# Stage 1 of a two-branch attention block: half a gate unit moved behind the scores, a z unit in the values' bank, the fourth query tile read and normalised last

## The chip, the cores and the metric

The kernel runs on one core of one Trainium2 chip. The metric is the time of one execution on the device in microseconds (us). The core has five engines, each with an instruction queue of its own: PE (TensorE, matmuls), DVE (VectorE), ACT (ScalarE), POOL (GpSimd) and SP (SyncE, which here issues DMAs). An engine takes its instructions in order; an instruction that waits for another engine holds all that stand behind it. Matmuls write to PSUM, which here has eight banks of 128 x 512 fp32.

## The reference

One decoder block: u is the normalised input; one projection of it gives the inputs of an MLA and a FoX attention (16 heads each), two z gates and two merge gates. 16 meta tokens stand ahead of 512 tokens. Cut to what matters:

```python
h = jnp.concatenate([meta_tokens, x], axis=1)                 # 528 positions, d_model 1024
u = rmsnorm(h, pre_norm_g[l])
proj = u @ w_in[l]
(cq, ckv, k_pe_raw, z_mla, fq, fk, fv, f_logit, z_fox, gate_a, gate_b) = jnp.split(proj, split_idx, axis=-1)
...
o_mla = causal_block_attention(q_m, k_m, v_mla, MLA_SCALE)
y_mla = (o_mla * jax.nn.silu(z_mla)) @ w_br_mla[l]
cum = jnp.cumsum(log_sigmoid(f_logit + fox_forget_b[l]), axis=-1)
o_fox = causal_block_attention(fox_heads(fq), fox_heads(fk), fox_heads(fv), FOX_SCALE, cum)   # + cum[t] - cum[s]
y_fox = (o_fox * jax.nn.silu(z_fox)) @ w_br_fox[l]
mixed = (jax.nn.sigmoid(gate_a) * y_mla + jax.nn.sigmoid(gate_b) * y_fox) @ w_out[l]
h = h + rmsnorm(mixed, post_norm_g[l])
return h[:, N_META:]
```

## The kernel before

Every fp32 product is made of three matmuls on split operands: an operand is written as a high part and a low part, and wh x uTh, wh x uTl and wl x uTh are summed in PSUM. A weight of a unit comes by DMA (`wraw`, 128 x 1024), ACT casts it to the high part (`wh`, L131), and a subtraction gives the low part (`wl`, L104), on POOL as a rule; in stage 1 alone two units have it on DVE (`low[0]=nc.vector` in the code). `wraw`, `wh` and `wl` have three buffers each.

After a start-up (norm, small projections, the values of the first pair) come 16 stages: for each of eight pairs of heads first FoX, then MLA. A stage computes the attention of its two heads; its free TensorE time is filled with units that later stages need. Units are named by their tile: `pg` is a merge gate (24 matmuls: eight steps of three), `z` a z gate (24), `mq` and `mk` MLA's queries and keys, `fq` and `fk` FoX's, `v` values. A `z` unit ends with ACT's tanh and a DVE product into `sil`, a `v` unit with two reductions on DVE (L698), a scale, and copies to `vh`.

Within a stage the work goes like this. PE makes the scores `st` of four query tiles of 128 (tile b has 144 + 128 b keys, so tile 3 is the largest): tile 1 and the first 240 keys of tile 3 share one pair of banks (one for each head), tile 0 and the rest of tile 3 the next, tile 2 has a pair alone. DVE evicts the scores to SBUF (`sf`), adding the bias or mask, and keeps a running minimum `nb` (L792; each eviction is followed by a read of its accumulator, shown as a second row with `nb` alone). ACT takes the exponentials and their sums `su` (L800). DVE scales and inverts the sums (L807, L808, into `ri`): a group of tiles 0 to 2 (six columns) and one of tile 3 (two). ACT writes the normalised high parts in f16 to `pn` (L826), DVE the low parts (L827), POOL the 16 meta columns (L813 to L818, by way of `mt`). SP issues four DMA transposes `pt<-pn`, one for a tile. When all four have landed, PE runs the 26 values matmuls `ov`, after the scores of the next stage.

PSUM's eight banks: three for `acc` (units, and tiles 1 and 3 of the scores), four by name (`b0`, `b1`, `c0`, `c1`: the rest of the scores, keys, values), one for `ov`.

PE's order is the order in which the code is written. That of the other engines is set by a scheduler when the kernel is built, from dependencies and priorities; `tc.high_priority` raises an instruction, and `tc.issue_after(x)` places what follows behind x. `weights(...)` splits each unit into a load, a preparation (`prep`: cast and subtraction) and the matmul steps, which `run(...)` writes out. Stage 1 (si == 0 in the code) is written by hand: gate unit, scores, z, then the rest.

Of the kernel before, what the change touches and what calls it, by code (L numbers as in the profile page):

```python
# [55 lines left out]
def block_kernel(ctx: ExitStack, tc: tile.TileContext, x, meta_tokens, pre_norm_g, w_in, fox_forget_b,  # L56
# [485 lines left out]
    with ExitStack() as att:  # L542
# [7 lines left out]
        def bank(tag):  # L550
            return lambda name: stp.tile([128, 512], F32, tag=tag, name=name)

        def two(tag):
            return lambda name: bank(tag + name[-1])(name)

# [18 lines left out]
        for b in range(4):  # L574
            nc.gpsimd.memset(pn[b // 3][:, PN_STEP * b % 15], 0.0)
        gT = []
        masks, normed = [], []

        wuqh = wuq.rearrange("p k (h e) -> p k h e", e=NOPE + ROPE)

# [148 lines left out]
        def z_unit(br, pr):  # L729
            def done(i, pz):  # L730
                sil = aw.tile([128, S], F32, tag="sil", name=f"sil{br}{pr}")
                with tc.high_priority(offset=60), nullcontext() if pr or not br else tc.issue_after(normed[0]):
                    ins = nc.scalar.activation(sil, pz, AF.Tanh, scale=0.5)
                    nc.vector.scalar_tensor_tensor(out=sil, in0=sil, scalar=1.0, in1=pz, op0=ALU.add, op1=ALU.mult)
                if written[0] and not br:

                    behind.append(ins.ins)
                sils[br, pr] = sil
            return unit(f"z{br}{pr}", win_w((O_ZM, O_ZF)[br], pr), u_act, KD, REAL, done)

        def attention(br, pr):


            scale = (SC_MLA, SC_FOX)[br]
            nm_ = f"{br}{pr}"
            q, k = hls["q", br, pr], hls["k", br, pr]

# [17 lines left out]
            def added(h, b, c0, c1):  # L765
# [3 lines left out]
                d = META + 128 * b if b else 0  # L769
                return [(a, e, cb[n][h][:, a:e]) for n, a, e in ((0, c0, min(c1, d)), (1, max(c0, d), c1)) if a < e]  # L770

            def scores():

                for t in ("nb", "su", "ri"):
                    sums[t] = aw.tile([128, 2, 4], F32, tag=t, name=f"{t}{nm_}")
                for g in range(2):
                    sfs[g] = aw.tile([128, 2, (2 * SF_STEP + 400, L)[g]], F32, tag=f"sf{g}", name=f"sf{nm_}{g}", bufs=1)
                for rooms, parts in (([acc, acc], ((1, 0, 272, 0), (3, 0, CUT, 272))),
                                     ([bank("b0"), bank("b1")], ((0, 0, 144, 0), (3, CUT, L - CUT, 144))),
                                     ([bank("c0"), bank("c1")], ((2, 0, 400, 0),))):  # L780
                    ps = [room(f"st{nm_}{parts[0][0]}{h}") for h, room in enumerate(rooms)]
                    for b, c0, w, o in parts:
                        for i, ops in enumerate(zip(*(sets(h, b, c0, w) for h in range(2)))):
                            for h, (Q, K) in enumerate(ops):
                                mm(ps[h][:, o : o + w], Q, K, start=(i == 0), stop=(i == last_set))
                    for b, c0, w, o in parts:
                        for h in range(2):
                            nb = sums["nb"][:, h, b : b + 1]
                            for a, e, in1 in added(h, b, c0, c0 + w):

                                with tc.high_priority(offset=100):
                                    nc.vector.tensor_tensor_reduce(  # L792
                                        out=sf_of(h, b)[:, a:e], in0=ps[h][:, o + a - c0 : o + e - c0],
                                        in1=in1, scale=-scale, scalar=3.0e38 if a == 0 else nb,
                                        op0=ALU.add, op1=ALU.min, accum_out=nb)
                with tc.high_priority(offset=60):
                    for b in (1, 0, 2, 3):
                        for h in range(2):
                            sf = sf_of(h, b)
                            exps[b // 3] = nc.scalar.activation(sf, sf, AF.Exp, bias=sums["nb"][:, h, b : b + 1],  # L800
                                                                scale=-1.0, accum_out=sums["su"][:, h, b : b + 1]).ins

            def norm(g):
                def fn():
                    b0, nb_ = GRP[g][0], len(GRP[g])
                    su, ri = (sums[t][:, :, b0 : b0 + nb_] for t in ("su", "ri"))
                    nc.vector.tensor_scalar(out=su, in0=su, scalar1=1.0 / PSCALE, scalar2=None, op0=ALU.mult)  # L807
                    nc.vector.reciprocal(ri, su)  # L808
# [4 lines left out]
                    nc.gpsimd.tensor_tensor(out=mt, in0=src, in1=ri.unsqueeze(3).broadcast_to([128, 2, nb_, META]),  # L813
                                            op=ALU.mult)
                    hi, lo, hi2 = (dst[:, :, :, 32 * i : 32 * i + META] for i in range(3))
                    nc.gpsimd.tensor_copy(hi, mt)
                    lead[:] = [nc.gpsimd.tensor_tensor(out=lo, in0=mt, in1=hi, op=ALU.subtract).ins]
                    nc.gpsimd.tensor_copy(hi2, mt)  # L818
                    for b in GRP[g]:
                        for h in range(2):  # L820
                            sf = sf_of(h, b)[:, META:].rearrange("p (j c) -> p j c", c=128)
                            t0 = PN_STEP * (b % 3) + 1
                            hi, lo = (pn[g][:, t0 : t0 + 2 * b + 2, h].rearrange("p (j l) c -> p j l c", l=2)[:, :, i]
                                      for i in range(2))
                            rib = sums["ri"][:, h, b : b + 1]
                            normed[:] = [nc.scalar.activation(hi, sf, AF.Copy, scale=rib).ins]  # L826
                            nc.vector.scalar_tensor_tensor(out=lo, in0=sf, scalar=rib, in1=hi, op0=ALU.mult,  # L827
                                                           op1=ALU.subtract)
                    for b in GRP[g]:
                        t0, n = PN_STEP * (b % 3), 2 * b + 3  # L830
                        dma(ptt[:, 0 : 2 * n, 128 * b : 128 * b + 128], pn[g][:, t0 : t0 + n].rearrange("p t h c -> p (t h c)"),
                            nc.sync.dma_start_transpose)
                return fn

            def values():
                po = ovp.tile([128, 512], F32, tag="ov", name=f"ov{nm_}")
# [93 lines left out]
        run(first[len(pe0) : -KD])  # L930
        behind[:] = [halved[("k", 1, 0), 1]]
        run(first[-KD:])
        behind.clear()
        late = []
        for si, (br, pr) in enumerate(stages):
# [6 lines left out]
                fn()  # L942
            if si == 0:

                run(fill[:1])
                run(vts[1, 0] + pe_rest)
                n0()
                bias(1)
                low[0] = nc.vector
                for ahead_ in [fn.prep for _, fn in fill[1:] if hasattr(fn, "prep")][:2]:  # L950
                    ahead_()
                low[0] = nc.gpsimd
                n1()
                run(fill[1:])
            else:
                if si == 1:
                    stores(2, 4)
# [361 lines left out]
```

## Time and profile before

| what | before |
|---|---|
| median of 3 runs | 590.39 us (590.29 to 591.79) |
| profiled execution | 589.93 us |
| its span, first to last instruction | 587.9 us |
| granted TensorE clock | 0.998 |
| PE busy | 577.0 us, 98% |
| DVE, ACT, POOL busy | 416.7, 357.2, 200.4 us |
| time of the chain that ended last on PE | 90% |

All times of single rows are microseconds from the start of the span of the profiled execution. A row of the timeline gives start, length, engine, line, operation, output <- inputs, shapes and how many instructions it stands for; brackets give the engine's idle time ahead of it and what ended it. A row with a count over 1 stands for neighbours, and its length is that from the first start to the last end. The two numbers after a tile name in the order listings are numbers of buffers and mean nothing else. Stage 1's scores start at 61.69 us and stage 2's at 77.93 us.

### The profile page before, as it was taken

How to read it: one execution, taken by the hardware profiler on the slowest of the kernel's cores; microseconds unless marked ns; L12 is line 12 of the kernel's file. 1: busy time of each engine (PE TensorE's matmuls, PEld its weight loads, DVE VectorE, ACT ScalarE, POOL GpSimd, SP SyncE). 2: the span in 40 equal slices, each digit the busy share in tenths (PEclk: the TensorE clock that was granted, in tenths of full speed). 3: DMA queues.
4: the chain of work that ended last, by engine and by line, in shares of the span. 5: the costliest groups of instructions: out<-in, count | busy, mean ns of one | idle time of the engine just before them, and what ended most of it. 6: DMA issues, size and time to landing. Idle time of an engine off the chain costs nothing.

```text
span 587.9 us, 11120 instructions
## 1 busy us (share of the span) xinstructions
PE 577.0 (98%) x3841; PEld 497.4 (85%) x3841; DVE 416.7 (71%) x1155; ACT 357.2 (61%) x816; POOL 200.4 (34%) x271
## 2 busy tenths in 40 slices
PE   8999989999999999999999999999999999999996
PEld 6889879889889889888898898878998998888884
DVE  5844687784885775766758758896747876468957
ACT  7846674783783784766748748844343462443663
POOL 4317736373467472554544644510000000000000
PEclk9999999999999999999999999999999999999999
DMA  8535399999978988988977977877622534333603
GB/s 291 127 81 168 88 194 195 234 189 277 171 169 161 223 189 204 218 190 203 178 175 178 226 149 146 183 174 259 207 73 71 144 108 130 86 109 107 216 0 143
DMA packets 219999, 97.46 MB, mean 166 GB/s; under 512 B 131456, under 2 KB 209672, under 8 KB 219944
## 3 DMA queue, kind: packets, MB, share of 16 engines
q1 hardware_dynamic: 219944, 96.77, 70.3%
q8 instruction: 30, 0.49, 0.3%
q14 instruction: 25, 0.20, 0.1%
HBM read 62.36 MB, written 3.97 MB: 113 GB/s over the span
## 4 chain that ended last, share of the span: by engine, by line
PE 90%; POOL 3%; DMA 2%; DVE 2%; ACT 1%; issue 1%; SPq 0%; DVEq 0%; POOLq 0%
PE z L98 17%; PE pg L98 14%; PE v L98 8%; PE x L98 8%; PE fq L98 8%; PE fk L98 8%; PE py L98 7%; PE st L98 7%; PE ov L98 5%; PE psm L98 3%; PE y L98 2%; PE mq L98 2%; POOL wl L104 1%; DMA pt<-pn 1%; PE mk L98 1%
## 5 line engine op out<-in xcount | busy, mean ns | idle before, releaser
L104 POOL TENSOR_TENSOR wl<-wraw,wh 128x1024 fp32r<-128x1024 f32 (+2 forms) x62 | 120.2, 1946 | 112.6 <-ACT wh L131 78.6
L131 ACT CAST wh<-wraw 128x1024 fp32r<-128x1024 f32 (+1 forms) x72 | 74.7, 1041 | 61.0 <-PE py L98 16.8
L800 ACT ACTIVATE sf<-sf,nb 128x272 f32<-128x272 f32 (+3 forms) x128 | 72.7, 569 | 10.9 <-DVE nb L792 10.1
L104 DVE TENSOR_TENSOR wl<-wraw,wh 128x512 fp32r<-128x512 f32 (+1 forms) x54 | 51.2, 950 | 31.9 <-ACT wh L1056 20.0
L827 DVE SCALAR_TENSOR_TENSOR pn<-sf,ri,pn 128x512 f16<-128x512 f32 (+3 forms) x128 | 71.5, 625 | 2.4 <-ACT pn L826 2.4
L826 ACT ACTIVATE pn<-sf,ri 128x512 f16<-128x512 f32 (+3 forms) x128 | 59.6, 548 | 0.0
L98 PE MATMUL z<-uTh,wh 128*128 128x512 f32 x128 | 51.1, 399 | 0.0
L98 PE MATMUL pg<-uTh,wh 128*128 128x512 f32 x128 | 50.1, 391 | 0.0
L98 PE MATMUL z<-uTl,wh 128*128 128x512 f32 x128 | 50.1, 391 | 0.0
L98 PE MATMUL z<-uTh,wl 128*128 128x512 f32 x128 | 50.0, 391 | 0.0
L98 PE MATMUL pg<-uTl,wh 128*128 128x512 f32 x128 | 49.9, 390 | 0.0
L98 PE MATMUL pg<-uTh,wl 128*128 128x512 f32 x128 | 49.8, 389 | 0.0
L98 PE MATMUL st<-hlk,hlq 64*128 64x272 f32 (+4 forms) x480 | 41.3, 299 | 0.0
L1056 ACT CAST wh<-wraw 128x512 fp32r<-128x512 f32 x28 | 17.3, 619 | 38.6 <-DVE wraw L1065 14.3
L698 DVE TENSOR_REDUCE vsc<-v 128x1 f32<-128x272 f32 (+1 forms) x32 | 13.1, 431 | 38.1 <-PE v L98 38.1
L98 PE MATMUL v<-uTh,wl 128*128 128x256 f32 (+1 forms) x128 | 36.5, 286 | 0.0
L98 PE MATMUL fk<-uTl,wh 128*128 128x256 f32 (+1 forms) x128 | 36.5, 285 | 0.0
L98 PE MATMUL v<-uTl,wh 128*128 128x256 f32 (+1 forms) x128 | 36.5, 285 | 0.0
L98 PE MATMUL fk<-uTh,wh 128*128 128x256 f32 (+1 forms) x128 | 36.4, 285 | 0.0
L98 PE MATMUL fk<-uTh,wl 128*128 128x256 f32 (+1 forms) x128 | 36.4, 285 | 0.0
L98 PEld LDWEIGHTS st<-hlk,hlq 64*128 64x128 f32 x480 | 33.0, 186 | 4.1 <-ACT vh L717 2.1
L98 PE MATMUL v<-uTh,wh 128*128 128x256 f32 (+1 forms) x128 | 36.4, 285 | 0.0
(285 smaller groups left out, 1611.6 us busy)
## 6 DMA issues: line engine op xcount, KB each, us to landing
wraw<-in_w_in_dram SPq DMA_DIRECT2D x56, 512.0 KB, 4.4
cbp<-c_dram SPq DMA_DIRECT2D x16, 264.0 KB, 3.7
wraw<-in_w_br_fox_dram SPq DMA_DIRECT2D x8, 512.0 KB, 4.3
tb<-in_w_out_dram SPq DMA_DIRECT2D x8, 512.0 KB, 5.2
wraw<-in_w_br_mla_dram SPq DMA_DIRECT2D x8, 512.0 KB, 4.2
wraw<-in_w_out_dram SPq DMA_DIRECT2D x6, 512.0 KB, 3.6
xr<-in_x_dram SPq DMA_DIRECT2D x4, 512.0 KB
out_dram<-yo SPq DMA_DIRECT2D x8, 256.0 KB, 2.0
```

The lines of the kernel that those rows point to most:

```text
L98: nc.tensor.matmul(*a, **k)
L104: return eng.tensor_tensor(out=lo, in0=src, in1=f32(hi), op=ALU.subtract)
L131: nc.scalar.copy(wh[:, :n], raw[:, :n])
L698: nc.vector.tensor_reduce(out=sc[:, i : i + 1], in_=ps, op=ALU.max, axis=AX.X, apply_absolute_value=True)
L800: exps[b // 3] = nc.scalar.activation(sf, sf, AF.Exp, bias=sums["nb"][:, h, b : b + 1], scale=-1.0, accum_out=sums["su"][:, h, b : b + 1]).ins
L826: normed[:] = [nc.scalar.activation(hi, sf, AF.Copy, scale=rib).ins]
L827: nc.vector.scalar_tensor_tensor(out=lo, in0=sf, scalar=rib, in1=hi, op0=ALU.mult, op1=ALU.subtract)
L1056: nc.scalar.copy(to[0], src)
```

## The change

Everything is in stage 1, and the computation is the same.

- Of the gate unit ahead of the scores only four of eight steps stay there; the other four (12 matmuls) run behind the scores, ahead of the unit z10.
- The unit z10 (FoX's z, first pair) takes the bank of `ov` instead of one of `acc`.
- DVE evicts tiles 1, 0 and 2 first (10 evictions). Tile 3's six evictions are placed behind the reciprocal of the first group, and its exponentials on ACT behind the last high copy of the first group.
- The weight subtraction of z00 (`wl`, on DVE) is placed behind the evictions of tiles 1, 0 and 2.

The core of the diff:

```diff
-            return unit(f"z{br}{pr}", win_w((O_ZM, O_ZF)[br], pr), u_act, KD, REAL, done)
+            room = ov_bank if br and not pr else None
+            return unit(f"z{br}{pr}", win_w((O_ZM, O_ZF)[br], pr), u_act, KD, REAL, done, room)
...
+            three_first = (br, pr) == stages[0]
...
+            def evict(places):
+                for b, c0, w, o, ps in places:
+                    for h in range(2):
+                        nb = sums["nb"][:, h, b : b + 1]
+                        for a, e, in1 in added(h, b, c0, c0 + w):
+
+                            with tc.high_priority(offset=100):
+                                ins = nc.vector.tensor_tensor_reduce(
+                                    out=sf_of(h, b)[:, a:e], in0=ps[h][:, o + a - c0 : o + e - c0],
+                                    in1=in1, scale=-scale, scalar=3.0e38 if a == 0 else nb,
+                                    op0=ALU.add, op1=ALU.min, accum_out=nb)
+                return ins.ins
...
+                    if three_first:
+                        places.extend(own)
+                    else:
+                        evict(own)
+                if three_first:
+                    whole[:] = [evict([p_ for p_ in places if p_[0] < 3])]
+                exponentials((1, 0, 2) if three_first else (1, 0, 2, 3))
...
-                    nc.vector.reciprocal(ri, su)
+                    inv = nc.vector.reciprocal(ri, su)
+                    if three_first and g == 0:
+                        with tc.issue_after(inv.ins):
+                            evict([p_ for p_ in places if p_[0] == 3])
...
+                    if three_first and g == 0:
+                        with tc.issue_after(normed[0]):
+                            exponentials((3,))
...
-        first = pe0 + v + [(0, in_order)] + g
+        first = pe0 + v + [(0, in_order)] + g[:4]
+        begun = g[4:]
...
-                fill = (vts[br, pr] if pr else []) + za + q + zb[:3] + k + zb[3:5] + v + zb[5:]
+                fill = (vts[br, pr] if pr else begun) + za + q + zb[:3] + k + zb[3:5] + v + zb[5:]
...
-                run(fill[:1])
+                run(fill[:5])
                 run(vts[1, 0] + pe_rest)
                 n0()
                 bias(1)
                 low[0] = nc.vector
-                for ahead_ in [fn.prep for _, fn in fill[1:] if hasattr(fn, "prep")][:2]:
-                    ahead_()
+                for ahead_ in [fn.prep for _, fn in fill[5:] if hasattr(fn, "prep")][:2]:
+                    with tc.issue_after(whole[0]):
+                        ahead_()
                 low[0] = nc.gpsimd
                 n1()
-                run(fill[1:])
+                run(fill[5:])
```

PE, around stage 1's scores (`pg` is the gate unit, `st` are scores, the number tells the bank's tile). Before, the last gate step and the first scores:

```order
L98 MATMUL pg_857<-uTh,wh_851 128x512
L98 MATMUL pg_857<-uTl,wh_851 128x512
L98 MATMUL pg_857<-uTh,wl_852 128x512
L98 MATMUL st_889<-hlk_653,hlq_619 128x272
L98 MATMUL st_890<-hlk_653,hlq_619 128x272
```

After, the last scores, the gate unit's fifth step behind them:

```order
L98 MATMUL st_903<-hlk_653,hlq_619 128x400
L98 MATMUL st_904<-hlk_653,hlq_619 128x400
L98 MATMUL pg_857<-uTh,wh_851 128x512
L98 MATMUL pg_857<-uTl,wh_851 128x512
L98 MATMUL pg_857<-uTh,wl_852 128x512
```

The four last steps of the gate unit have moved from ahead of the 30 score matmuls to behind them; z10 follows.

DVE in stage 1, from the last evictions on (L792 is L786 after, L807/L808 are L828/L829, L827 is L851, L734 is L737). Before, where `wl_1005` of z00 stands ahead of all evictions and so is not among these rows:

```order
L792 ISA sf_887,nb_884<-st_929,cbm_707,nb_884 128x128
L792 ISA nb_884 128x1
L807 TENSOR_SCALAR su_885<-su_885 128x2
L808 RECIPROCAL ri_886<-su_885 128x2
L807 TENSOR_SCALAR su_885<-su_885 128x2x3
L808 RECIPROCAL ri_886<-su_885 128x2x3
L827 SCALAR_TENSOR_TENSOR pn_716<-sf_888,ri_886,pn_716 128x4x128
L827 SCALAR_TENSOR_TENSOR pn_715<-sf_887,ri_886,pn_715 128x128 x2
L827 SCALAR_TENSOR_TENSOR pn_715<-sf_887,ri_886,pn_715 128x2x128 x2
L827 SCALAR_TENSOR_TENSOR pn_715<-sf_887,ri_886,pn_715 128x3x128 x2
L827 SCALAR_TENSOR_TENSOR pn_716<-sf_888,ri_886,pn_716 128x4x128
L734 SCALAR_TENSOR_TENSOR sil_1041<-sil_1041,z_955 128x512
```

After, from the last eviction of tile 3 on; the reciprocal of the first group (128x2x3) stands ahead of tile 3's six evictions:

```order
L786 ISA sf_874,nb_870<-st_890,cbm_708,nb_870 128x128
L786 ISA nb_870 128x1
L104 TENSOR_TENSOR wl_1005<-wraw_855,wh_1004 128x1024
L851 SCALAR_TENSOR_TENSOR pn_715<-sf_873,ri_872,pn_715 128x128 x2
L851 SCALAR_TENSOR_TENSOR pn_715<-sf_873,ri_872,pn_715 128x2x128 x2
L851 SCALAR_TENSOR_TENSOR pn_715<-sf_873,ri_872,pn_715 128x3x128 x2
L828 TENSOR_SCALAR su_871<-su_871 128x2
L829 RECIPROCAL ri_872<-su_871 128x2
L104 TENSOR_TENSOR hlq_1053<-mq_1046,hlq_1053 128x512
L851 SCALAR_TENSOR_TENSOR pn_716<-sf_874,ri_872,pn_716 128x4x128 x2
L737 SCALAR_TENSOR_TENSOR sil_1041<-sil_1041,z_947 128x512
L104 TENSOR_TENSOR hlk_1072<-mk_1068,hlk_1072 128x272
```

The subtraction for z00 has gone from ahead of the evictions to behind them, and tile 3 (sf_874, pn_716 after) is normalised last, behind the low part of hlq.

More of the change, by code (lines that the diff above doesn't have):

```diff
@@ L551, in bank, with ov_bank @@
             return lambda name: stp.tile([128, 512], F32, tag=tag, name=name)
+        def ov_bank(name):
+            return ovp.tile([128, 512], F32, tag="ov", name=name)
         def two(tag):
@@ L576, in block_kernel @@
         gT = []
-        masks, normed = [], []
+        masks, normed, whole = [], [], []
         wuqh = wuq.rearrange("p k (h e) -> p k h e", e=NOPE + ROPE)
@@ L770, in added @@
                 return [(a, e, cb[n][h][:, a:e]) for n, a, e in ((0, c0, min(c1, d)), (1, max(c0, d), c1)) if a < e]
+            places = []
+            def evict(places):
[9 more added lines that the diff above has]
+                return ins.ins
             def scores():
@@ L781, in scores @@
                     ps = [room(f"st{nm_}{parts[0][0]}{h}") for h, room in enumerate(rooms)]
+                    own = []
                     for b, c0, w, o in parts:
+                        own.append((b, c0, w, o, ps))
                         for i, ops in enumerate(zip(*(sets(h, b, c0, w) for h in range(2)))):
@@ L785, in scores, with exponentials @@
                                 mm(ps[h][:, o : o + w], Q, K, start=(i == 0), stop=(i == last_set))
[L786 to L795, printed above, removed]
+                    if three_first:
[5 more added lines that the diff above has]
+                exponentials((1, 0, 2) if three_first else (1, 0, 2, 3))
+            def exponentials(bs):
                 with tc.high_priority(offset=60):
-                    for b in (1, 0, 2, 3):
+                    for b in bs:
                         for h in range(2):
@@ L835, in values @@
             def values():
-                po = ovp.tile([128, 512], F32, tag="ov", name=f"ov{nm_}")
+                po = ov_bank(f"ov{nm_}")
                 ph = [po[64 * h : 64 * h + 64] for h in range(2)]
@@ L929, in block_kernel @@
         gT += [gpool.tile([128, KD, S], F32, tag=n, name=n) for n in ("gT0", "gT1")]
-        run(first[len(pe0) : -KD])
+        run(first[len(pe0) : -4])
         behind[:] = [halved[("k", 1, 0), 1]]
-        run(first[-KD:])
+        run(first[-4:])
         behind.clear()
```

## The prediction

> **What bounds the kernel now.** I read the busy totals first, then the chain that ended last, then TensorE's waits in the stretch that the change touches (60 to 140 us from the span's start), and last the rows around those waits. The first line gives each engine's busy time, the second the shares of the chain, the third TensorE's waits in that stretch (total us, times, longest).
>
> ```profile
> PE 577.0 (98%) x3841; PEld 497.4 (85%) x3841; DVE 416.7 (71%) x1155; ACT 357.2 (61%) x816; POOL 200.4 (34%) x271
> PE 90%; POOL 3%; DMA 2%; DVE 2%; ACT 1%; issue 1%; SPq 0%; DVEq 0%; POOLq 0%
> PE ov L98 <- DMA pt<-pn: 2.2, 1, 2.2
> 81.17 0.35 PE L98 MATMUL st<-KPL,QP 64*128 64x400 f32 x2
> 83.73 2.04 PE L98 MATMUL ov<-pt,vp 80*64 80x512 f16 x26 [2.21 <-DMA pt<-pn]
> 124.57 0.35 PE L98 MATMUL st<-KPL,QP 64*128 64x400 f32 x2
> 124.84 2.04 PE L98 MATMUL ov<-pt,vp 80*64 80x512 f16 x26
> ```
>
> TensorE is the bound: it is busy 98% of the span, so a faster side engine is worth only the TensorE idle time that it ends. In 80 us that is a single wait: stage 1's values matmuls (ov) start at 83.73 because a transpose pt<-pn lands late. What it costs is read against the same join two stages later, which waits for nothing: there ov starts 0.27 us after the last score row (124.84 - 124.57), here 2.56 us after it (83.73 - 81.17). The excess, **2.29 us**, is all that this change can win by ending that wait.
>
> Now why the transpose is late. TensorE runs the gate unit, then the scores, then z. The last row, of the chain, is the flight of the last transpose (issue, us to landing).
>
> ```profile
> 56.13 0.40 PE L98 MATMUL pg<-uTh,wh 128*128 128x512 f32 x1
> 58.87 0.39 PE L98 MATMUL pg<-uTh,wh 128*128 128x512 f32 x1
> 61.69 2.26 PE L98 MATMUL st<-hlk,hlq 64*128 64x272 f32 x30
> 63.88 0.50 PE L98 MATMUL z<-uTh,wh 128*128 128x512 f32 x1
> 61.61 1.05 ACT L131 CAST wh<-wraw 128x1024 fp32r<-128x1024 f32 x1 [2.98 <-PE pg L98]
> 62.69 1.36 DVE L104 TENSOR_TENSOR wl<-wraw,wh 128x1024 fp32r<-128x1024 f32 x1 [3.32 <-ACT wh L131]
> 63.98 0.29 DVE L792 CUSTOM_DVE_ANT_0 sf<-st,cbp 128x144 f32<-128x144 f32 x1
> 68.97 0.08 DVE L792 DVE_READ_ACCUMULATOR2_ANT nb<- 128x1 f32 x1
> 68.28 0.72 ACT L800 ACTIVATE sf<-sf,nb 128x528 f32<-128x528 f32 x1
> 70.57 0.19 DVE L808 RECIPROCAL ri<-su 128x6 f32<-128x6 f32 x1
> 70.23 3.72 ACT L826 ACTIVATE pn<-sf,ri 128x512 f16<-128x512 f32 x8
> 70.97 3.99 DVE L827 SCALAR_TENSOR_TENSOR pn<-sf,ri,pn 128x512 f16<-128x512 f32 x8 [0.21 <-ACT pn L826]
> 74.22 0.74 DVE L827 SCALAR_TENSOR_TENSOR pn<-sf,ri,pn 128x512 f16<-128x512 f32 x1
> 77.59 6.00 DMA pt<-pn
> ```
>
> The scores end at 63.88, yet the first eviction starts only at 63.98, behind z00's weight split (wl, 62.69 to 64.05). Sixteen evictions run to 69.05, the reciprocal for tiles 0 to 2 ends at 70.76, hi and lo copies to 74.96, and the last transpose, issued at 77.59, lands 6.00 us later.
>
> **The change part by part.**
>
> *Half a gate unit behind the scores.* Twelve of 24 matmuls move: 58.87 - 56.13 = 2.74 us of TensorE work. The scores start at 61.69 - 2.74 = 58.95 and the order before and after holds the same rows, so z still starts at 63.88; on TensorE itself this costs nothing. Where scores meet waiting values the first eviction follows by 1.10 us:
>
> ```profile
> 103.11 2.26 PE L98 MATMUL st<-hlk,hlq 64*128 64x272 f32 x30
> 104.21 0.31 DVE L792 CUSTOM_DVE_ANT_0 sf<-st,cbp 128x144 f32<-128x144 f32 x1 [0.17 <-PE st L98]
> ```
>
> So the first eviction falls at 60.05, 3.93 us earlier than now. 2.74 of that is the move, the rest the weight split that stood ahead.
>
> *Tiles 1, 0 and 2 first.* Before, from first eviction to the end of that reciprocal went 70.76 - 63.98 = 6.78 us, with tile 3's two exponentials in it (0.72 each). Without them: 60.05 + 6.78 - 1.44 = 65.4; tile 3's six evictions also leave the front of DVE's queue, so this is a late bound. ScalarE then casts wh (1.05) and does the gate's tanh, 0.59 by the next row: 67.0 if none overlaps, 66.6 if the cast follows the last exponential directly. Six of the eight hi copies, about 2.5 of the 3.72 us, end at about 69.2; two exponentials with their reads take 1.5 more (70.7); hlq's cast waits for mq's last matmul at 70.99 and ends at 71.6; tile 3's two hi copies (0.6 to 0.7) end at about 72.9.
>
> ```profile
> 62.56 0.59 ACT L538 ACTIVATE th<-pg 128x512 f32<-128x512 f32 x1
> 70.60 0.39 PE L98 MATMUL mq<-cTh,wl 128*128 128x512 f32 x1
> 70.83 0.40 PE L98 MATMUL z<-uTh,wh 128*128 128x512 f32 x1
> 75.48 0.68 DVE L104 TENSOR_TENSOR hlq<-mq,hlq 128x512 fp32r<-128x512 f32 x1
> 76.76 0.76 DVE L698 TENSOR_REDUCE vsc<-v 128x1 f32<-128x272 f32 x2
> 75.65 0.28 PE L98 MATMUL v<-cTh,wl 128*128 128x256 f32 x1
> ```
>
> On DVE: six evictions from 65.4 at 5.07/16 = 0.32 each, to 67.3; the split wl 1.36, to 68.7; six lo copies at about 0.4, to 71.2; two small ones; hlq's lo (0.68) to 72.3; tile 3's two lo copies (0.74 each) to 73.8. The last transpose is issued at about 73.8 instead of 77.59 and lands at 79.8. Values are wanted at 83.73 - 2.29 = 81.44: **the 2.29 us end**, with 1.6 us to spare.
>
> *z10 in the values' bank; late frees.* Tile 3's scores hold their banks until 67.3, and the gate unit its own until its tanh. The next units that need one start at 70.83 (z00) and later, so this is hidden. The split wl, now after the evictions, is ready at 68.7 against the same 70.83: 2.1 us of cover; if that goes, TensorE waits at z00, one for one. The values at 81.44 come well behind z10's reading from that bank. SP's and POOL's rows are the same in number; POOL's four small operations on tiles 0 to 2 come ahead of tile 3's and wait for no more than they did.
>
> *What is late next.* Stage 2's values weights. DVE's backlog of stage 1 now delays v's second reduction: TensorE ends v at 75.93, the two reductions end at 77.52, and a chain of DVE and ScalarE steps leads from there to stage 2's first eviction and its reciprocals:
>
> ```profile
> 80.59 0.43 DVE L792 CUSTOM_DVE_ANT_0 sf<-st,maskt 128x272 f32<-128x272 f32 x1
> 84.99 0.17 DVE L808 RECIPROCAL ri<-su 128x2 f32<-128x2 f32 x1
> 85.30 0.24 POOL L813 TENSOR_TENSOR mt<-sf,ri 128x32 f32<-128x32 f32 x1 [2.04 <-DVE ri L808]
> 87.59 2.40 POOL L104 TENSOR_TENSOR wl<-wraw,wh 128x1024 fp32r<-128x1024 f32 x1
> 89.96 0.80 POOL L813 TENSOR_TENSOR mt<-sf,ri 128x96 f32<-128x96 f32 x1
> 91.81 2.58 POOL L104 TENSOR_TENSOR wl<-wraw,wh 128x1024 fp32r<-128x1024 f32 x1
> 94.21 0.29 PE L98 MATMUL v<-uTh,wh 128*128 128x272 f32 x1
> 94.46 0.38 PE L98 MATMUL v<-uTh,wl 128*128 128x272 f32 x1
> 87.58 2.97 DVE L827 SCALAR_TENSOR_TENSOR pn<-sf,ri,pn 128x512 f16<-128x512 f32 x1 [0.62 <-ACT pn L826]
> ```
>
> After the change DVE has caught up by then, so the second reduction (the later half of the 0.76 row) can start right behind v, about 75.97 against about 77.1: **1.11 us earlier**, and with it the eviction (79.48), the reciprocal (84.05) and POOL. From 85.30 POOL works without a gap to 94.39 and ends with the wl of stage 2's v unit. TensorE's third v matmul needs that wl: its row is 0.38 long where its neighbour takes 0.29, so it already waits 0.09. With the stall gone TensorE would be there at 94.46 - 2.29 = 92.17; POOL, 1.11 earlier, would have wl at 93.28, usable at about 93.44 (the old one ended at 94.39 and was used from 94.55, the 0.09 counted, so 0.16 later). A new wait of about 1.27 us opens at v.
>
> **Sum:** -2.29 (values' wait) + 1.27 (new wait at v) - 0.09 (the old one, in it) = -1.11 us. The profiled execution took 589.93 us, so one like it would take 588.8; the median of the runs shown is 590.39, 0.46 above, and there the forecast is 590.39 - 1.11 = **589.3 us**. The unknown in it is how far stage 2's chain moves. Below: not at all, if DVE's backlog stays, which gives no gain. Above: the eviction cannot come before the scores that it reads, which bounds the move to about 1.2 us, and POOL's rows can shorten. I take 1.11, the nearer end: between 74.96 and the second reduction at about 77.1 DVE had 2.1 us of work, of which hlq's lo (0.6 net) is done earlier after the change, so from 73.8 it is through at about 75.3, 0.6 us ahead of v's end.
>
> [...] In the last row above a lo copy of DVE took 2.97 us beside POOL's wl split (87.59, 2.40), against 0.74 for the same shape at 74.22. [...]
>
> **The rivals.**
>
> *Nearly the full gain.* If POOL's stretch shortens as well, the new wait at v shrinks. For it: in that stretch mt's 0.80 is slow beside DVE's copies; the same operation took 0.35 in stage 1:
>
> ```profile
> 70.91 0.35 POOL L813 TENSOR_TENSOR mt<-sf,ri 128x96 f32<-128x96 f32 x1 [0.39 <-DVE ri L808]
> ```
>
> That is 0.45, and 0.18 for wl at 2.40 instead of 2.58: 0.63 us, so 588.7. With no wait at v at all it would be 590.39 - 2.29 = 588.1. Against it: the same neighbours run together after the change, only shifted as a block.
>
> *No gain.* The transposes or DVE's work of stage 1 stay late by 2 us or more, or the whole of stage 2's chain hangs on something that does not move; TensorE then regains at the values what it gives back at v: 590.4. Against it: v's reductions wait for DVE alone in the rows above.
>
> *Slower: DVE and POOL lock each other in stage 1.* The split wl and eight lo copies now run from about 67 on, beside POOL's operations on tiles 0 to 2. If each of the eight lost as much as the longest of POOL's small rows there, 0.61 (pn's copy at 71.32), that is 4.9 us of DVE delay:
>
> ```profile
> 71.32 0.61 POOL L816 CAST pn<-mt 128x96 f16<-128x96 f32 x1
> ```
>
> Slack ahead of v's reduction is 0.6 us, and 1.11 of gain is to be lost first: from 1.7 us of delay on it is slower than before, from 3.5 by over 0.3%, and at 4.9 us it would be 590.39 + 3.2 = 593.6. Against it: POOL has only some 2 us of such work in all, and before the change it ran beside the same copies, which still came to 3.99 us for eight.
>
> **How the numbers follow.** Chances: forecast 0.50, nearly the full gain 0.26, no gain 0.10, slower 0.14. The likeliest's own range is 588.7 to 590.0 (a move of stage 2's chain between 0.4 and 1.2, with POOL up to 0.5 shorter). The 8-in-10 range reaches below to just under the full gain, 587.9, and above over the case without gain to 590.8; what it leaves out is most of the slower case. 0.3% of 590.4 is 1.77 us, about what a measurement of this kernel can tell from no change: the faster side is most of the second case, 0.25; the slower side most of the last one and a little for what I have not seen, 0.15; the rest, 0.60, is between.
>
> **What would show each step.** In the changed profile: scores at about 58.95 and the first eviction at about 60.05; wl of z00 on DVE behind the evictions; the last of stage 1's four transposes landing near 79.8 and no wait of ov, which starts near 81.4; stage 2's two-wide reciprocal near 84.05; TensorE's v matmul waiting about 1.2 us for POOL's wl near 92.2; stage 3's scores at about 102.0 instead of 103.11. Wrong would make it: a wait of TensorE at z00 near 70.8 for wl or a bank, lo copies in stage 1 much longer than 0.74, ov still waiting, or POOL's stretch of another length than 9.1 us.

## The result, and the profile after

The changed kernel takes 589.13 us (median of 7 runs, 588.78 to 589.51), the kernel before, run beside it, 591.15 (7 runs, 590.29 to 591.79). The ratio is 0.9974, with a 95% interval of 0.9964 to 0.9984: 1.5 us less, between 0.9 and 2.1; the two medians are 2.0 us apart. The profiled execution took 589.07 us against 589.93. Of the kernel before, one run beside the last experiments took 3271.22 us and is left out everywhere.

The page of the changed kernel, span and busy time:

```profile
span 587.1 us, 11116 instructions
PE 577.8 (98%) x3841; PEld 497.7 (85%) x3841; DVE 419.4 (71%) x1155; ACT 357.1 (61%) x816; POOL 199.0 (34%) x271
```

TensorE is still busy 98% of the span. The chain that ended last can be followed back only to 83.91 us in this profile, so its shares are not set beside those of before. TensorE's waits between 60 and 140 us, and its rows around them:

```profile
PE v L98 <- POOL wl L104: 1.1, 1, 1.1
56.31 0.40 PE L98 MATMUL pg<-uTh,wh 128*128 128x512 f32 x1
59.15 2.26 PE L98 MATMUL st<-hlk,hlq 64*128 64x272 f32 x30
61.34 0.50 PE L98 MATMUL pg<-uTh,wh 128*128 128x512 f32 x1
81.36 0.34 PE L98 MATMUL st<-KPL,QP 64*128 64x400 f32 x2
81.63 2.04 PE L98 MATMUL ov<-pt,vp 80*64 80x512 f16 x26
92.14 0.29 PE L98 MATMUL v<-uTh,wh 128*128 128x272 f32 x1
93.61 0.39 PE L98 MATMUL v<-uTh,wl 128*128 128x272 f32 x1 [1.06 <-POOL wl L104]
102.27 2.26 PE L98 MATMUL st<-hlk,hlq 64*128 64x272 f32 x30
```

The values matmuls now start 0.27 us after the last score row, and a new wait stands at stage 2's v unit, for POOL's weight split. The gate unit starts 0.18 us later than in the profile of before (56.31 against 56.13), which is start-up and not the change. Counted from that row, stage 3's scores start after 45.96 us instead of 46.98: **1.02 us** gained, and from there on both kernels run alike.

DVE, POOL and SP in stages 1 and 2 of the changed kernel:

```profile
60.17 0.31 DVE L786 CUSTOM_DVE_ANT_0 sf<-st,cbp 128x144 f32<-128x144 f32 x1 [0.60 <-PE st L98]
64.57 0.84 DVE L828 TENSOR_SCALAR su<-su 128x6 f32<-128x6 f32 x1 [1.13 <-ACT sf L821]
65.45 0.19 DVE L829 RECIPROCAL ri<-su 128x6 f32<-128x6 f32 x1
67.33 1.22 DVE L104 TENSOR_TENSOR wl<-wraw,wh 128x1024 fp32r<-128x1024 f32 x1
68.46 2.46 DVE L851 SCALAR_TENSOR_TENSOR pn<-sf,ri,pn 128x128 f16<-128x128 f32 x6
72.46 1.41 DVE L851 SCALAR_TENSOR_TENSOR pn<-sf,ri,pn 128x512 f16<-128x512 f32 x2
74.78 3.00 SPq L92 DMA_TRANSPOSE pt<-pn  x1
75.80 0.78 DVE L701 TENSOR_REDUCE vsc<-v 128x1 f32<-128x272 f32 x2 [0.65 <-PE v L98]
79.71 0.44 DVE L786 CUSTOM_DVE_ANT_0 sf<-st,maskt 128x272 f32<-128x272 f32 x1
84.14 0.17 DVE L829 RECIPROCAL ri<-su 128x2 f32<-128x2 f32 x1
84.48 0.24 POOL L837 TENSOR_TENSOR mt<-sf,ri 128x32 f32<-128x32 f32 x1 [2.13 <-DVE ri L829]
91.00 2.55 POOL L104 TENSOR_TENSOR wl<-wraw,wh 128x1024 fp32r<-128x1024 f32 x1
86.73 10.58 DVE L851 SCALAR_TENSOR_TENSOR pn<-sf,ri,pn 128x512 f16<-128x512 f32 x8 [0.60 <-ACT pn L850]
```

Stage 1's last transpose is issued at 74.78 instead of 77.59; v's reductions wait 0.65 us for TensorE, where before DVE came to them 0.83 us after v's end (76.76 against 75.93); and POOL's stretch of stage 2 runs from 84.48 to 93.55, 9.07 us without a long gap (9.09 before).

### The profile page after: what moved, and what is told of

The parts are those of the page before. It is cut to its first block, busy times and chain, and to the rows that moved or that the text cites. A ratio compares the mean times of both kernels' runs of the same rounds, so it can differ in the third digit from the quotient of the medians.

```text
span 587.1 us, 11116 instructions
## 1 busy us (share of the span) xinstructions
PE 577.8 (98%) x3841; PEld 497.7 (85%) x3841; DVE 419.4 (71%) x1155; ACT 357.1 (61%) x816; POOL 199.0 (34%) x271
## 4 chain that ended last, share of the span: by engine, by line
PE 83%; POOL 1%; issue 0%; DVE 0%; DVEq 0%; ACT 0%; POOLq 0%
PE z L98 17%; PE pg L98 14%; PE v L98 8%; PE x L98 8%; PE py L98 7%; PE st L98 7%; PE fk L98 6%; PE fq L98 6%; PE ov L98 5%; PE y L98 2%; PE mq L98 2%; PE mk L98 1%; POOL wl L104 1%; PE ppe L98 0%; POOL mt L837 0%
## 5 line engine op out<-in xcount | busy, mean ns | idle before, releaser
L851 DVE SCALAR_TENSOR_TENSOR pn<-sf,ri,pn 128x512 f16<-128x512 f32 (+3 forms) x128 | 73.6, 641 | 2.1 <-ACT pn L850 1.9
L850 ACT ACTIVATE pn<-sf,ri 128x128 f16<-128x128 f32 (+3 forms) x128 | 59.7, 548 | 0.0
```

## The experiments

My theory was the prediction's: the wait at ov is worth 2.29 us, stage 2's chain moves 1.1 us, and TensorE gives the difference back at v. The rivals were that one part alone does it, or that the two waits have nothing to do with each other. Each ratio is to runs of the kernel before on the same chip; the medians of different rows are in part of different chips. Start-up differs from one profiled execution to the next by up to 1.4 us (the gate unit started between 56.03 and 57.45), so beside the ratios this table gives, from the traces, the time from the gate unit's start to stage 3's and to stage 5's scores:

| kernel | to stage 3 | to stage 5 | median us | runs, us | ratio to before (95%) |
|---|---|---|---|---|---|
| before, profile shown above | 46.98 | 88.02 | 591.15 | 590.29 to 591.79 | 1 |
| before again | 48.53 | 89.57 | 590.66 | 589.75 to 592.78 | 1.0003 (0.9992 to 1.0014) |
| changed | 45.96 | 87.00 | 589.13 | 588.78 to 589.51 | 0.9974 (0.9964 to 0.9984) |
| changed again | 45.97 | 87.01 | 589.03 | 588.89 to 589.60 | 0.9972 (0.9961 to 0.9983) |
| half gate unit alone | 46.35 | 87.39 | 589.66 | 589.14 to 590.06 | 0.9978 (0.9969 to 0.9987) |
| tile 3 last alone | 45.96 | 87.00 | 589.09 | 588.75 to 589.88 | 0.9972 (0.9963 to 0.9982) |
| changed, fk ahead of v | 44.63 | 86.32 | 588.52 | 588.33 to 589.18 | 0.9964 (0.9951 to 0.9976) |
| changed, z10 in acc | 47.88 | 88.92 | 591.06 | 590.65 to 591.26 | 0.9994 (0.9984 to 1.0005) |
| before, later transpose | 49.21 | 90.25 | 592.92 | 591.13 to 596.76 | 1.0033 (1.0016 to 1.0051) |
| changed, later transpose | 47.64 | 89.00 | 592.48 | 591.32 to 593.61 | 1.0022 (1.0009 to 1.0035) |
| changed, v's split on DVE | 44.62 | 85.73 | 588.67 | 587.97 to 589.79 | 0.9959 (0.9944 to 0.9974) |
| tile 3 last, v's split on DVE | 45.14 | 88.66 | 589.34 | 588.21 to 591.46 | 0.9978 (0.9966 to 0.9989) |

**The kernel before again.** No edit.

> The kernel before once more, unchanged, for the spread of its runs and a second profile. The wait at stage 1's values hangs on a DMA's flight, which may differ from run to run. If that is why the runs before lie up to 1.5 us apart, the second profile shows another flight and another wait at ov (first: 6.00 us and 2.21 us) while all before ov agrees within 0.3 us. Rival: the spread is in the start-up or the tail, and the wait at ov is 2.2 us again. Ratio 1.000 either way.

The flight of the last transpose and the wait at ov were the same to 0.03 us; the idea that the DMA's flight makes the spread fell. But the second half of the rival did not hold alone either. The chain's row of that transpose, and TensorE's rows at ov:

```profile
78.93 6.01 DMA pt<-pn
85.08 3.30 PE L98 MATMUL ov<-pt,vp 80*64 80x512 f16 x26 [2.24 <-DMA pt<-pn]
```

The same 26 matmuls took 3.30 us instead of 2.04. Windows around the end of the wait, first of the profile of before, then of this one, cut where its clock changes (busy time of PE, its weight loads, DVE, ACT and POOL with counts; then the granted clock, the DMA share and GB/s):

```profile
83.00:86.00 3.00, 2.27 (x27) 1.82 (x28) 1.71 (x8) 3.00 (x11) 0.89 (x5) 1.00 1.15 342
86.00:89.00 3.00, 3.00 (x15) 2.45 (x14) 2.36 (x4) 3.00 (x7) 3.00 (x6) 1.00 1.80 105
```

```profile
82.26:85.67 3.41, 1.17 (x14) 0.69 (x12) 3.41 (x20) 3.16 (x11) 2.36 (x1) 1.00 0.84 218
85.67:89.08 3.41, 3.41 (x26) 2.61 (x21) 1.26 (x6) 3.24 (x8) 2.34 (x9) 0.50 0.75 218
89.08:92.49 3.41, 3.41 (x17) 2.82 (x16) 3.41 (x5) 3.19 (x8) 3.35 (x4) 1.00 1.38 72
```

The granted clock was 0.50 for 3.41 us where it had been 1.00, and counted from the gate unit stage 3's scores came 1.55 us later. This execution took 592.78 us, 2.85 above the other profiled one: about 1.5 from the lower clock, 1.32 in the start-up (57.45 against 56.13).

**Half the gate unit alone.** Tile 3 in the old order; z00's preparation is not tied to the evictions.

```diff
-            three_first = (br, pr) == stages[0]
+            three_first = False
...
-                    with tc.issue_after(whole[0]):
-                        ahead_()
+                    ahead_()
```

> Only the half gate unit behind the scores and z10 in the values' bank; all 16 evictions, exponentials and copies in the old order. My theory: scores near 59.1 are early enough by themselves, so ov's wait is gone; but z00's weight split now comes behind six lo copies on DVE and is ready at about 71.9 instead of 68.6, so TensorE waits about 0.5 us at z00, v's end and with it stage 2's chain are 0.5 us later, and the gain against the kernel before is about 0.5 us (ratio 0.999) instead of the full change's. Rival: tile 3 last is what ends the wait at ov; then ov waits here still for 1 us or more.

TensorE's waits in this kernel between 50 and 140 us:

```profile
PE v L98 <- POOL wl L104: 1.0, 1, 1.0
PE z L98 <- DVE wl L104: 0.2, 1, 0.2
```

ov no longer waits, z00 waits a little for its split (0.17 us in its row; stage 2's scores start 0.44 later than in the others), and stage 3 comes 0.63 us sooner than before, 0.39 later than with the whole change. The mechanism is the expected one; the rival, that tile 3's order is needed to end the wait, is out. The ratio, 0.9978, shows more gain than the 0.999 expected; the trace's 0.63 us is near the expected 0.5. What the runs have beyond the traces comes up below, with the clock.

**Tile 3 last alone.** The whole gate unit ahead of the scores.

```diff
-        first = pe0 + v + [(0, in_order)] + g[:4]
-        begun = g[4:]
+        first = pe0 + v + [(0, in_order)] + g
+        begun = []
...
-            room = ov_bank if br and not pr else None
+            room = None
```

(and the numbers that count steps, 5 back to 1 and 4 back to KD)

> Only tile 3 read and normalised last and z00's split behind the evictions; the whole gate unit ahead of the scores, z10 in a bank of acc. The scores are at 61.7 to 61.9 again. My theory: tile 3's lo copies end at about 75 and the last transpose lands at 80 to 82, so ov waits 0 to 0.6 us; DVE ends stage 1's work at about 76.2, some 0.2 to 0.5 us after v's end, so stage 2's chain gains 0.6 to 0.9 of the 1.1 us. Gain against before 0.6 to 1.0 us (ratio 0.9983 to 0.999). Rival: without the earlier scores nothing is won, ov waits as before for about 2.2 us and the ratio is 1.000.

```profile
PE v L98 <- POOL wl L104: 0.9, 1, 0.9
```

That is TensorE's only wait listed there; ov starts 0.43 us behind the last score row instead of 0.27, so that 0.16 us of its wait is left. The gain to stage 3 is the whole 1.02 us, a little over what I expected, and the ratio, 0.9972, is below the expected 0.9983 to 0.999. So each half of the change ends the wait at ov by itself, or all but 0.16 us of it, and the half gate unit adds nothing measurable to the other: what is left is set behind ov, at v. This kernel holds two edits, tile 3's order and z00's split behind the evictions; which of them it takes was not tried.

**fk's matmuls ahead of v.** In stage 2 alone, 12 matmuls of fk's second half run ahead of v.

```diff
-                fill = vts[br, pr] + q + k[:KD] + v + k[KD:]
+                n_ = KD + (4 if si == 1 else 0)
+                fill = vts[br, pr] + q + k[:n_] + v + k[n_:]
```

> The changed kernel, and in stage 2 alone half of fk's second half (12 matmuls, about 1.5 us) runs ahead of the v unit instead of behind it. My theory: what the change leaves is the 1.2 us wait of v's third matmul for POOL's weight split; with 1.5 us of other work ahead the split is in time, the wait is gone and the kernel is 1.0 to 1.2 us faster than the changed one (ratio to before 0.9955 to 0.996), unless the last transpose of stage 2, which lands about 0.2 us ahead of when values would then be wanted, becomes the next wait (then 0.3 to 0.8 us less). Rival: the wait only moves to the next unit that needs stage 2's chain, stage 3's scores or values, and the time is that of the changed kernel (ratio 0.9974).

The wait at v is gone, and stage 3's scores start 1.33 us sooner than in the changed kernel. But 0.65 of it is lost at once, and not where I looked for it (PEld are TensorE's weight loads):

```profile
101.21 2.85 PE L98 MATMUL st<-hlk,hlq 64*128 64x272 f32 x30
102.86 0.86 PEld L98 LDWEIGHTS st<-hlk,hlq 64*128 64x128 f32 x8 [0.31 <-DVE hlk L104]
102.39 0.41 DVE L104 TENSOR_TENSOR hlk<-fk,hlk 128x256 fp32r<-128x256 f32 x1
102.72 0.47 DVE L723 SCALAR_TENSOR_TENSOR vh<-v,vsc,vh 128x256 f16<-128x256 f32 x1
```

The 30 score matmuls take 2.85 us instead of 2.26. The keys' low part, done on DVE at 102.80, now comes while the scores run, and a weight load waits 0.31 us for it. The rest of the loss falls around the end of v's last copy on DVE, 103.19; that the copy is its cause is argued from this time alone. The rival was half right: half of the gain is lost at stage 3's scores, and to stage 5 0.68 us are left.

**z10 in a bank of acc.**

```diff
-            room = ov_bank if br and not pr else None
+            room = None
```

> The changed kernel with z10 back in a bank of acc. The gate unit and tile 3's scores then hold all three banks of acc when TensorE comes to z10 at about 64 us. My theory: z10 waits for the gate's tanh, which in the changed kernel ends at about 66.0, so TensorE idles some 2 us at z10; half of it comes back since the wait at v (1.1 us) shrinks, but v's end and stage 2's chain are later too, so the time is 1 to 2.5 us above the changed kernel (ratio to before 0.999 to 1.002). Rival: the bank is free in time and the values' bank was not needed; ratio 0.9974.

```profile
PE z L98 <- DVE nb L786: 1.7, 1, 1.7
PE v L98 <- POOL wl L104: 1.1, 1, 1.1
66.07 0.47 PE L98 MATMUL z<-uTh,wh 128*128 128x512 f32 x1 [1.67 <-DVE nb L786]
```

z10 waits. The profile names an eviction of tile 3, whose accumulator was read by 65.92; the gate's tanh, which I had expected, ended at 66.03, and the two are not separated. Stage 3 comes 1.92 us later than in the changed kernel: all of the wait and a little more, nothing of it comes back at v, since the delay at z10 lies ahead of v's own reductions and moves stage 2's chain with it. The values' bank is what lets the half gate unit move at no cost on TensorE.

**A later transpose, before and after.** Tile 0's transpose is issued once more (in the kernel before) or twice more (in the changed one) ahead of tile 3's, the same data to the same place.

```diff
-                    for b in GRP[g]:
+                    for b in ((0,) * 1 if br and not pr and g else ()) + GRP[g]:
```

> The kernel before, with tile 0's transpose issued a second time ahead of tile 3's in stage 1, which delays the last transpose by about 1.3 us and so lengthens TensorE's wait at ov from 2.2 to about 3.5 us. The second profile of the kernel before showed a granted clock of 0.61 for some 3 us behind the 2.2 us wait, where the first showed 1.00, and 1.54 us more to stage 3's scores. My theory: an idle stretch of 2 to 2.5 us sometimes lowers the clock, and a longer one does so more often: then nearly all runs lie 2.5 to 3.1 us above the faster half of the runs of before (about 590.1), without a second cluster 1.3 us lower. Rival: the lower clock is chance and not tied to the wait; then the runs lie 1.0 to 1.6 us above before and spread as before.

> The changed kernel with tile 0's transpose issued two more times ahead of tile 3's, so that the last transpose is issued at about 77.5 as in the kernel before, while DVE and stage 2's chain stay as early as in the changed one. My theory: ov waits again for 1.3 to 2.2 us, but then TensorE comes later to v, whose wait of 1.1 us for POOL's split shrinks to between 0 and 0.3; net 0.3 to 1.1 us above the changed kernel (ratio to before 0.998 to 1.0). Rival: the two waits add up, 1.3 to 2.2 us above the changed kernel with v's wait as long as there (ratio 1.000 or more).

TensorE's rows at ov and the windows behind, first of the kernel before with the later transpose, then of the changed kernel with it, there with ScalarE's first weight cast behind stage 2's exponentials:

```profile
84.43 3.48 PE L98 MATMUL ov<-pt,vp 80*64 80x512 f16 x26 [2.90 <-DMA pt<-pn]
84.84:88.25 3.41, 3.41 (x25) 2.58 (x22) 0.83 (x4) 2.81 (x6) 2.74 (x9) 0.50 0.94 281
```

```profile
84.26 2.04 PE L98 MATMUL ov<-pt,vp 80*64 80x512 f16 x26 [2.19 <-DMA pt<-pn]
84.00:87.00 3.00, 2.74 (x29) 2.17 (x29) 1.21 (x4) 1.50 (x6) 2.09 (x8) 1.00 0.96 257
87.14 1.05 ACT L131 CAST wh<-wraw 128x1024 fp32r<-128x1024 f32 x1 [1.65 <-DMA wraw<-in_w_in_dram]
95.65 0.39 PE L98 MATMUL v<-uTh,wl 128*128 128x272 f32 x1 [0.48 <-POOL wl L104]
```

In the first the wait grew to 2.90 us, less than I meant, and the clock was 0.50 for 3.41 us behind it; the median rose by 1.5 us (591.43 for the kernel before on that chip, 592.92 here), and only one of 12 runs lay under 592.2. That fits the expectation's size only in part: 7 of the 12 runs, not nearly all, have a mean granted clock of 0.995 or less, and the runs reach 596.76, further up than either theory said. The extra transpose also delays the weight loads behind it on SP (the first of them was issued at 82.53 instead of 81.00). In the second the wait at ov came back with 2.19 us and the one at v shrank from 1.06 to 0.48, not to nothing, and the ratio, 1.0022, is above the expected 0.998 to 1.0. The trace shows why: SP's later weight loads make ScalarE wait 1.65 us at its cast, which stands ahead of the copies and splits of stage 2. Counted from the gate unit, ov starts 2.26 us later than in the changed kernel and POOL's split for v comes 1.67 us later, so only 0.58 comes back. The edit thus moved both sides of v and does not by itself show that a loss at ov alone comes back in full; the changed kernel's second execution, below, shows it for a small one.

**v's split on DVE.** In stage 2 alone, v's weights are cast and split ahead of the copies, the split on DVE.

```diff
                 n1()
+                if si == 1:
+                    low[0] = nc.vector
+                    with tc.high_priority(offset=30):
+                        fill[17][1].prep()
+                    low[0] = nc.gpsimd
```

> The changed kernel, with the weight split of stage 2's v unit on DVE and cast and split ahead of the hi and lo copies instead of on POOL behind them. My theory: TensorE's wait at v goes (split done before 92 us), and DVE's lo copies, stretched to 10.6 us beside POOL's splits, shorten by 2 us or more, as one POOL split less runs beside them; 0.9 to 1.3 us below the changed kernel (ratio to before 0.9953 to 0.996). Rival: ScalarE waits at that cast for the weights, which land at about 89, and the hi copies, the transposes and stage 2's values come later than they are wanted; then it is no faster than the changed kernel or slower (0.9974 or more).

```profile
86.77 3.20 DVE L104 TENSOR_TENSOR wl<-wraw,wh 128x1024 fp32r<-128x1024 f32 x1 [0.93 <-ACT wh L131]
89.89 4.06 DVE L851 SCALAR_TENSOR_TENSOR pn<-sf,ri,pn 128x128 f16<-128x128 f32 x8
86.48 2.41 POOL L104 TENSOR_TENSOR wl<-wraw,wh 128x1024 fp32r<-128x1024 f32 x1
84.76 1.98 ACT L131 CAST wh<-wraw 128x1024 fp32r<-128x1024 f32 x2
```

No wait of TensorE is left between 50 and 140 us. ScalarE did both casts without a gap, the second from about 85.7 on, where the rival had the weights landing at about 89: it is out. The split on DVE took 3.20 us beside POOL's (1.22 in stage 1 of the changed kernel), but then the eight lo copies took 4.06 us, not 10.58. Stage 5 comes 1.27 us sooner than in the changed kernel; this is the fastest of the kernels by trace, though its runs spread over 1.8 us and its interval still meets the changed kernel's.

**Tile 3 last and v's split on DVE, without the gate move.** The two edits above together.

> Tile 3 read and normalised last, the gate unit whole ahead of the scores and z10 in acc, and the weight split of stage 2's v on DVE ahead of the copies. The half gate unit behind the scores added nothing to stage 3's start (45.96 us behind the gate unit's start with it and without it). My theory: it adds nothing here either, stage 3's scores start 44.6 us behind the gate unit's start as in the kernel with all three parts and the v split, and the time is 1.0 to 1.4 us below the changed kernel's. Rival: the earlier scores are needed once v no longer waits; ov or stage 3's scores then wait and the gain over the changed kernel is under 0.7 us.

```profile
PE ov L98 <- DMA pt<-pn: 2.8, 2, 2.4
81.92 2.04 PE L98 MATMUL ov<-pt,vp 80*64 80x512 f16 x26 [0.47 <-DMA pt<-pn]
105.83 2.04 PE L98 MATMUL ov<-pt,vp 80*64 80x512 f16 x26 [2.37 <-DMA pt<-pn]
92.77 11.00 SPq L92 DMA_TRANSPOSE pt<-pn  x4
75.39 6.39 DMA pt<-pn
```

The rival was right in this execution: 0.47 us is lost at ov in stage 1 and 2.37 in stage 2. In stage 1 TensorE comes to ov no sooner than with tile 3 last alone (the last score row 25.04 us behind the gate unit's start in both); the last transpose lands later (the last row, of the chain: issued at 75.39, 6.39 us in flight). In stage 2 TensorE is early, v's wait being gone, and SP needs 11.00 us for the four transposes, from 92.77 on (9.45 us, from 91.31 on, with the gate move). SP had ended stage 1's transposes at 78.81 instead of 77.67, and all that stands behind them in its queue comes later; why stage 2's also took longer I did not separate. The half gate unit, worth nothing beside the wait at v, is worth 2.93 us to stage 5 in these two executions (88.66 against 85.73) once that wait is gone. But this one took 590.82 us, and the runs here spread from 588.21 to 591.46; by the medians, which are of different chips, it is 0.7 us, and the intervals of the two ratios overlap.

**The changed kernel again.** No edit.

> The changed kernel once more, beside the next one on the same chip. If the lower clock behind the wait at ov is why the runs of the kernel before fall into two groups (about 590.0 and 591.5 us), the runs of this one, whose longest idle stretch after the start-up is 1.1 us, stay within 1 us of each other, with a median near 589.1 and a profile with granted clock 1.00 around ov and v. Rival: the two groups come from the chip or the start-up, and show here too.

```profile
81.72 2.04 PE L98 MATMUL ov<-pt,vp 80*64 80x512 f16 x26
93.50 0.39 PE L98 MATMUL v<-uTh,wl 128*128 128x272 f32 x1 [0.89 <-POOL wl L104]
```

The runs stayed within 0.71 us, with 1.00 granted in all windows around ov and v, beside runs of the kernel before on the same chip between 590.17 and 592.04, so the chip alone does not make the spread.

The two rows show the give-back. In this execution ov starts 25.52 us behind the gate unit's start, 0.20 later than in the first one, with the last score row where it was; the wait at v is 0.89 instead of 1.06, and stage 3 comes after 45.97 instead of 45.96. What is lost at ov came back at v. With tile 3 last alone it was the same: ov 0.15 later, the wait at v 0.93, stage 3 after 45.96.

## Why the prediction was right

- **The scores and evictions:** 58.95 and 60.05 were predicted, 59.15 and 60.17 came, with the 0.18 of start-up in them.
- **Tile 3 last:** the reciprocal of the first group was expected at 65.4 and ended at 65.64. Two errors cancel in it: the exponentials ended sooner, and the small scaling of the sums ahead of it took 0.84 us where I had the 0.2 of before in the sum. The split wl ended at 68.55 (68.7), the last lo copy at 73.87 (73.8). These times too have the 0.18 of start-up in them.
- **The last transpose** was issued 1.0 us later than I said (74.78 for 73.8), since SP was busy with the three ahead of it until 74.26, which I had not counted; in the profile of before too it was issued 2.63 us after the last lo copy (77.59 against 74.96). It landed at 79.78 by the trace's landing marks, just where I said, since the flight took 5.00 us and not 6.00. That the two errors cancel is luck, and the 1.6 us of spare time that I saw are not there in every execution: in the second one of the changed kernel the last part of this transpose landed at 81.58, and ov started 0.20 us late.
- **Stage 2's chain:** 1.11 us earlier was predicted. The eviction came at 79.71 (79.48 plus the 0.18), the reciprocal ended at 84.31 (84.05 plus it), POOL's stretch took 9.07 us (9.1): 1.00 to 1.06 us earlier than before, net of start-up.
- **The new wait at v** was predicted as 1.27 us beyond the normal pace; between the first and the third v matmul lie 1.47 us (93.61 - 92.14) where it was 0.25 before (94.46 - 94.21), so 1.22. **Stage 3's scores** came at 102.27 for 102.0, 0.18 of it start-up.
- **The total:** -1.11 by the sum, -1.02 by the trace from the gate unit on, -0.86 between the two profiled executions. By all runs it is -1.5 (0.9 to 2.1). What the sum lacks is in part what the wait at ov did in some executions of the kernel before: the clock dropped behind it, for about 1.5 us more. The sum was made on an execution in which it did not. But the 62 runs of before without a low mean clock (last section) have a median of 590.47, 1.3 above the changed kernel's 589.13; the 0.3 between that and the trace's 1.02 stay open. That the time came within 0.2 us of the 589.3 is in part luck: the forecast started from 590.39, the middle of three runs, and from the 591.15 of all seven the same sum gives 590.0.
- **The rivals:** the nearly full gain did not come, since POOL's stretch kept its length (9.07 us for 9.09); mt on tiles 0 to 2 took 0.80 us again and ran, like the other small rows, beside the same copies. The slower case took for each of stage 1's eight lo copies a loss of 0.61 us, the length of a POOL row. No run shows that term: before, with POOL's rows on tiles 0 to 2 beside them, the eight took 3.99 us; in the changed kernel, where those rows had ended at 67.26, ahead of the first copy at 68.46, they took 3.87. In stage 2, with POOL's splits beside some of them, the eight took 8.42 us before and 10.58 after.
- **Not seen:** that either half of the change would have ended the wait at ov by itself. The prediction costed them as one chain and never asked how much of it was needed: the gain is capped at about 1 us by v, and either half reaches that or most of it.

## What to carry to other kernels

When a wait on the bounding engine ends, work out when the engine will then want the next thing that it takes from the slow side, and how far that moved: the gain is the smaller of the two shifts, here 1.0 of 2.3 us. A part that adds nothing today can be what the next fix needs (the half gate unit was worth nothing with the wait at v; without it 0.7 us by medians, not clear of noise, and more in the one pair of traces), so test parts alone and again behind the next fix. And price an idle stretch of TensorE like the 2.2 us here above its length: in 28 of the 90 runs of the kernel before some 1.2 us more went with it (a median of 591.69 against 590.47).

## What the runs showed of the hardware

An idle stretch of TensorE may cost more than itself. Behind a wait of 2.24 us in one profiled execution, and behind 2.90 us in another, the granted clock was 0.50 for 3.41 us; in the 3.41 us ahead of the drop TensorE had been busy for 1.17 us in the first and 0.51 in the second. Behind waits of 2.21, 2.19 and 2.37 us in three others, and 1.67 in one, it stayed 1.00.

Only one or two executions of each kernel have a profile, but the mean granted clock of the changed kernel's runs and of all runs beside the experiments is on record, and one such drop is 0.003 of it (half of 3.41 us in 588). Of 90 runs of the kernel before 28 have a mean of 0.995 or less; their median is 591.69 us, that of the other 62 is 590.47. Of the 60 runs of the six kernels with no wait over 1.7 us none has 0.995 or less. So the drop goes with the wait, and comes in about a third of the runs of the kernel before. It is not the whole spread: the 62 lie between 589.53 and 592.04, and the 12 runs of the kernel with tile 3 last and v's split on DVE spread over 3.25 us without one such mean. Kernels with no wait over 1.7 us spread over 0.6 to 1.2 us (one, with v's split on DVE, over 1.8), those with 2.2 us or more over 1.5 to 5.6.

DVE's lo copies were slow beside POOL's splits of 128 x 1024. The same eight copies took 3.87 us in stage 1 and 10.58 in stage 2 of the changed kernel. There three of them ran beside such splits and took 3.00, 2.72 and 2.75 us; the other five took 0.40 to 0.74 each. With v's split moved to DVE ahead of them no copy started beside a POOL split, and the eight took 4.06. Whether the scaling of 0.84 us, which also ran beside a POOL split, has the same cause was not tried.
